# An LRU layer's first blocks fed by chunks of the norm, with the adaLN sums moved behind them

## The chip, the cores and the metric

The kernel runs on one core of one Trainium2 chip. The metric is the device time of one execution in microseconds (us). Of three executions the median was 2819.17 us (2819.03 to 2819.62).

## The reference, cut to what matters

Two layers over 1024 latent tokens and 256 context tokens, width 1024: an RG-LRU mixer, then a Hyena mixer, each followed by a squared-ReLU MLP of width 4096. The change touches the first layer's start, and for a few lines the preparation of the Hyena filters. What is computed there:

```python
mod = cond @ ada_w[0] + ada_b[0]           # six parts: sh1, sc1, g1, sh2, sc2, g2
u = rms_norm(x) * g * (1 + sc1) + sh1      # x: 1024 tokens; the same for the 256 of ctx
z = u @ w_in + b_in                        # 1024 -> gate half and xl half
gate = gelu(z[:, :W]);  xl = conv4(z[:, W:])
r, i = sigmoid(xl_head @ w_a + b_a), sigmoid(xl_head @ w_i + b_i)   # two directions, heads of 256
a = exp(-8 r softplus(-lam));  bx = sqrt(1 - a^2) * i * xl
h = scan(a, bx) in both directions, started from the context's last state
x = x + g1 * (((h_f + h_b) * gate) @ w_out + b_out)
x = x + g2 * mlp(rms_norm(x) * g' * (1 + sc2) + sh2)
```

## The kernel before

Activations stand transposed: channels on the 128 partitions, tokens along the free dimension, in three chunks (0 and 1: 512 latent tokens each, 2: the 256 context tokens). Each product in float32 is made as three matmuls of a rounded part and a remainder (`mm3`, L133): high by high, high by low, low by high. `load` (L111) brings a weight block of 128x1024 by SP's DMA queue into one of two `raw` buffers, ScalarE rounds it into `whi` (L115), VectorE makes the remainder `wlo` (L117). The same two `raw` buffers also take other weights, in program order.

Each instruction's engine is fixed by the code; the order on an engine comes from a planner that simulates the program when it is built (`schedule_with_timeline_sim`), with `high_priority` blocks first. On the chip each engine then works in that fixed order, and an instruction that waits holds up all behind it on its engine. `tc.issue_after(ins)` puts what the block traces behind `ins` on the engine of `ins`, in order only.

The start of the program, in the order of the code:
- `ada_first` (L161) makes the parts 0 and 1 of `mod` (shift and scale of the first norm) for latent and context together: for each part eight blocks of 512 KB of `ada_w`, two matmuls a block with only two weight columns (L174), a row of 2x1024 copied out by ScalarE (L179), eight small transposes (L181), two additions (L183, L184). It is called from `aside` (L1178), between the three rounds of `filter_pos` (L318, the Hyena filter's small network on VectorE and ScalarE). Between the two parts `x_load` brings all of x and ctx, and `norm_stats` works out the three chunks' norms.
- the end of `filter_pos` shuffles the network's output into `hp`, splits it and writes it to DRAM (`hpd`); `filter_w4` (L370) splits 1 MB of `fw4` and writes it to DRAM (`w4d`), for `filters` (L376) to fetch four times in the MLP.
- `lru` (L478) applies the norm, chunk by chunk (`norm_apply`, L282: VectorE L288, ScalarE L290, ScalarE's rounding L291, remainder L292 on GpSimd for even and VectorE for odd blocks).
- then the tokens of L473, one after another. X makes one block of 128 channels of xl (24 matmuls for each chunk, then a convolution on VectorE L527, rounding L547 and remainder L549), Z one block of the gate, U both gates of both directions (it needs both X of its head), A and S the coefficients and the scans, Y fetches finished blocks back for w_out. E (L652) sums one whole part of `mod` on VectorE: eight blocks of 512 KB through `raw`, one multiplication and seven multiply-adds of 128x1024 (L659, L661), then small matmuls (L664).

```python
TOKENS = ("X00 X01 E20 Z00 E30 U00 E40 A00 X10 S00 Z01 U01 A01 X11 S01 "
```

So the first two X, the parts 2, 3 and 4 of `mod`, the first Z and the first U alternate, and every E stands in the same SP queue, `raw` buffers and VectorE and TensorE queues as the blocks around it.

Of the kernel before, what the change touches and what calls it, by code (L numbers as in the profile page):

```python
# [16 lines left out]
P = 128  # L17
# [29 lines left out]
def tile_block(ctx: ExitStack, tc: tile.TileContext, a, out, dbg=None):  # L47
# [49 lines left out]
    w4d = dram.tile([4, P, 2, 512], F32, name="w4d")  # L97
# [64 lines left out]
    def ada_first(pool, wpool):  # L162

        pp = {}

        def step(j, k):
            tag = ("raw", "hi", "lo", "hi", "lo", "raw", "hi", "lo")[k]
            w = wpool.tile([P, 1024], F32R if tag != "raw" else F32, tag=tag, name=nm("afw"), bufs=2 if tag == "raw" else 3)
            w = w.bitcast(F32) if tag != "raw" else w
            nc.sync.dma_start(w, a["ada_w"][0, k * P:(k + 1) * P, j * D:(j + 1) * D])  # L170
            if k == 0:
                pp[j] = [psum(), psum()]
            for h in range(2):
                nc.tensor.matmul(pp[j][h][0:2, :], cond[:, :, k], w[:, h * 512:(h + 1) * 512], start=(k == 0), stop=(k == NT - 1))  # L174
            if k == NT - 1:
                pt = psum()
                for h in range(2):
                    row = pool.tile([P, 512], F32, tag="acc", name=nm("arow"), bufs=1)[0:2]
                    nc.scalar.copy(row, pp[j][h][0:2, :])  # L179
                    for t in range(4):  # L180
                        nc.tensor.transpose(pt[:, 8 * h + 2 * t:8 * h + 2 * t + 2], row[:, t * P:(t + 1) * P], ident[0:2, 0:2])  # L181
                pv = pt[:, 0:16].rearrange("p (t a) -> p t a", a=2)
                nc.vector.tensor_tensor(mod[:, 0, j], pv[:, :, 0], vcols("ada_b", 8 * j, 8), op=ALU.add)  # L183
                nc.vector.tensor_tensor(modc[:, j], pv[:, :, 1], vcols("ada_b", 8 * j, 8), op=ALU.add)  # L184
        return [lambda j=j, k=k: step(j, k) for j in range(2) for k in range(NT)]
# [94 lines left out]
    applied = [None, None]  # L280

    def norm_apply(pool, xs, r, n, scale, shift, uh, ul, inplace=False):  # L282

        rb = r if r.shape[-1] == n else norm_bcast(pool, r, n, 1 if inplace else 2)
        for k in range(NT):
# [4 lines left out]
            nc.scalar.activation(u, t, AF.Identity, scale=scale[:, k:k + 1], bias=shift[:, k:k + 1])  # L290
            nc.scalar.copy(uh[k], u)  # L291
# [26 lines left out]
    def filter_pos(fp, fb, aside):  # L318
# [13 lines left out]
        for n in range(3):  # L332
# [12 lines left out]
            aside(n)  # L345
        tap("fh3", h)
# [8 lines left out]
        hp = fp.tile([P, 16, 4, 32], F32, tag="hp", name="hp")  # L355
        nc.gpsimd.memset(hp, 0.0)
        for half in range(2):
# [5 lines left out]
            for m in range(2):  # L363
                for j in range(4):
                    eng = nc.scalar.copy if j % 2 else nc.vector.tensor_copy
                    eng(dst[:, :, m, (j + m) % 4, 16 * half:16 * half + 16], src[:, :, m, j, :])
        for n, t in enumerate(split(fb, "hps", hp.rearrange("p g j t -> p (g j t)"), [P, 2048], 1, "v")):
            nc.sync.dma_start(hpd[:, :, n].rearrange("g p c -> p g c"), t.bitcast(F32).rearrange("p (g c) -> p g c", g=16))

    def filter_w4(fp, fb):  # L370
        fw4 = fp.tile([P, 2048], F32, tag="fw4", name="fw4")
        nc.sync.dma_start(fw4, a["fw4"])
        for n, t in enumerate(split(fb, "w4s", fw4, [P, 2048], 1)):
            nc.sync.dma_start(w4d[:, :, n].rearrange("u p c -> p u c"), t.bitcast(F32).rearrange("p (u c) -> p u c", u=4))

    def filters(fp):  # L376
# [88 lines left out]
    def x_load(pool):  # L465
        xt = []
        for c, src, o, n in ((0, "xT", 0, 512), (1, "xT", 512, 512), (2, "ctxT", 0, TC)):
            xt.append([pool.tile([P, n], F32, tag=f"x{c}{k}", name=nm("xl"), bufs=1) for k in range(NT)])
            for k in range(NT):
                nc.sync.dma_start(xt[c][k], a[src][k * P:(k + 1) * P, o:o + n])  # L470
        return xt
# [946 lines left out]
```

## Time and profile before

| | |
|---|---|
| median of three executions | 2819.17 us |
| the profiled execution's own time | 2820.53 us |
| its span | 2818.8 us (1.7 us lie around it) |
| TensorE busy | 2664.5 us, 95% |
| VectorE busy | 1519.5 us, 54% |
| ScalarE busy | 1045.7 us, 37% |
| GpSimd busy | 256.6 us, 9% |
| mean granted TensorE clock | 0.97 of full speed |

The profile is one execution. Engines are PE (TensorE, with PEld its weight loads), DVE (VectorE), ACT (ScalarE), POOL (GpSimd) and SP (the queue that issues most DMAs). A matmul's time in the trace is longer than its distance to the next, since they are pipelined; the distance is what counts. "ps L135 <- ACT u L291" says that a matmul of line 135 waited for the ScalarE instruction of line 291.

### The profile page before, as it was taken

Reading aid. Unit: us, or ns where it says so; the run is one execution under the profiler, and the core shown is the slowest. Engines: PE = TensorE matmul, PEld = TensorE weight load, DVE = VectorE, ACT = ScalarE, POOL = GpSimd, SP = SyncE. Lnnn points to the kernel's source line nnn. Section 1 sums busy time; section 2 is a strip of 40 time slices with the busy share of each in tenths; the row PEclk is TensorE's granted clock in tenths of the full one; section 3 lists DMA queues with packets and bytes.
Section 4 is the critical chain, followed back from the end, with each engine's and each line's share of the span. In section 5 each row is a group of like instructions: output and inputs, shape, how many; then the busy total and the mean of one; then the engine's idle time right before and its main releaser. Section 6 shows DMA issues by size and latency. Waiting matters only on the chain. (4 is left out here: it accounts for less than half of the span.)

```text
span 2818.8 us, 30100 instructions
## 1 busy us (share of the span) xinstructions
PE 2664.5 (95%) x11578; PEld 2027.9 (72%) x11578; DVE 1519.5 (54%) x2077; ACT 1045.7 (37%) x1566; POOL 256.6 (9%) x162
## 2 busy tenths in 40 slices
PE   6689898999999999999999998889799999999998
PEld 1577777878777777778787763333588888888887
DVE  7665665874554554554843447547485333333336
ACT  5557577552333333322622233323353221112213
POOL 0223333010000000000100013212000000000000
PEclk8789999999999999999999999999999999999999
DMA  8331122342443443431313235555421111111112
GB/s 302 124 123 40 50 75 100 117 129 75 135 134 114 142 133 110 135 114 57 120 56 111 83 123 150 139 162 160 134 83 48 51 47 51 45 53 45 53 45 97
DMA packets 120272, 286.28 MB, mean 102 GB/s; under 512 B 11898, under 2 KB 27900, under 8 KB 120002
## 3 DMA queue, kind: packets, MB, share of 16 engines
q1 hardware_dynamic: 109618, 261.30, 29.5%
q10 hardware_dynamic: 8256, 14.68, 1.8%
q0 software_dynamic: 2256, 8.39, 0.9%
q8 instruction: 91, 1.49, 0.2%
q14 instruction: 51, 0.42, 0.0%
HBM read 212.76 MB, written 37.75 MB: 89 GB/s over the span
## 5 line engine op out<-in xcount | busy, mean ns | idle before, releaser
L154 PE MATMUL ps<-u,whi 128*128 128x512 f32 x2696 | 733.5, 392 | 0.0
L115 ACT CAST whi<-raw 128x1024 fp32r<-128x1024 f32 x206 | 216.7, 1052 | 1130.8 <-PE ps L154 1033.5
L154 PEld LDWEIGHTS ps<-u,whi 128*128 128x128 f32 x2696 | 504.1, 188 | 114.6 <-DVE x L789 4.2
L117 DVE TENSOR_TENSOR wlo<-raw,whi 128x1024 fp32r<-128x1024 f32 x206 | 262.1, 1272 | 468.7 <-ACT whi L115 467.9
L154 PE MATMUL ps<-u,wlo 128*128 128x512 f32 x1348 | 421.3, 389 | 0.1
L154 PEld LDWEIGHTS ps<-u,wlo 128*128 128x128 f32 x1348 | 252.9, 188 | 53.7 <-DVE wlo L117 0.8
L154 PE MATMUL ps<-hh,whi 128*128 128x512 f32 x896 | 290.6, 393 | 0.0
L154 PE MATMUL ps<-hh,wlo 128*128 128x512 f32 x896 | 288.4, 389 | 0.0
L154 PE MATMUL ps<-hl,whi 128*128 128x512 f32 x896 | 287.7, 390 | 0.0
L154 PEld LDWEIGHTS ps<-hh,whi 128*128 128x128 f32 x896 | 168.2, 188 | 51.4 <-DVE x L789 11.1
L136 PE MATMUL ps<-u,whi 128*128 128x512 f32 (+1 forms) x508 | 195.4, 386 | 3.7 <-POOL u L292 3.1
L135 PE MATMUL ps<-u,whi 128*128 128x512 f32 (+1 forms) x508 | 187.3, 385 | 11.5 <-ACT u L291 11.5
L137 PE MATMUL ps<-u,wlo 128*128 128x512 f32 (+1 forms) x508 | 193.1, 382 | 1.8 <-DVE wlo L117 1.8
L154 PEld LDWEIGHTS ps<-hh,wlo 128*128 128x128 f32 x896 | 168.1, 188 | 35.2
L154 PEld LDWEIGHTS ps<-hl,whi 128*128 128x128 f32 x896 | 167.9, 188 | 33.8
L789 DVE SCALAR_TENSOR_TENSOR big<-ps,mod,big 128x512 f32<-128x512 f32 (+1 forms) x132 | 91.7, 731 | 185.2 <-PE ps L154 177.7
L789 DVE SCALAR_TENSOR_TENSOR x<-ps,mod,x 128x512 f32<-128x512 f32 x128 | 91.4, 747 | 132.8 <-PE ps L154 124.9
L415 DVE TENSOR_TENSOR ht<-ps,ht 128x512 f32<-128x512 f32 x64 | 44.0, 687 | 162.9 <-PE ps L137 162.9
L292 POOL TENSOR_TENSOR u<-nu,u 128x512 fp32r<-128x512 f32 x24 | 33.9, 1412 | 990.6 <-ACT u L291 981.4
L135 PEld LDWEIGHTS ps<-u,whi 128*128 128x128 f32 x508 | 98.0, 194 | 30.1 <-ACT u L291 12.3
L136 PEld LDWEIGHTS ps<-u,whi 128*128 128x128 f32 x508 | 98.2, 193 | 25.6 <-POOL u L292 6.4
L137 PEld LDWEIGHTS ps<-u,wlo 128*128 128x128 f32 x508 | 97.7, 192 | 20.3 <-DVE wlo L117 3.0
(228 smaller groups left out, 3798.2 us busy)
## 6 DMA issues: line engine op xcount, KB each, us to landing
raw<-in_mlp_w_dram SPq DMA_DIRECT2D x136, 512.0 KB
adaw<-in_ada_w_dram SPq DMA_DIRECT2D x112, 256.0 KB
fd<-fe SPq DMA_DIRECT2D x64, 256.0 KB
ft<-fd SPq DMA_DIRECT2D x64, 256.0 KB
e<-big SPq DMA_DIRECT2D x64, 256.0 KB
eraw<-in_ada_w_dram SPq DMA_DIRECT2D x24, 512.0 KB
raw<-in_hy_w_in_dram SPq DMA_DIRECT2D x24, 512.0 KB
big<-e ACTq DMA_DIRECT2D x48, 256.0 KB
```

What stands on the lines that cost most here:

```text
L115: lsplit[0] = nc.scalar.copy(hi, raw)
L117: lsplit[1] = nc.vector.tensor_tensor(lo, raw, hi.bitcast(F32), op=ALU.subtract)
L135: first = pin(nc.tensor.matmul(ps, wh, rh, start=start, stop=False))
L136: pin(nc.tensor.matmul(ps, wh, rl, start=False, stop=False))
L137: pin(nc.tensor.matmul(ps, wl, rh, start=False, stop=stop))
L154: nc.tensor.matmul(pp[c], x, y[c][k], start=first, stop=last)
L292: applied[k % 2] = (nc.vector if k % 2 else nc.gpsimd).tensor_tensor(ul[k], u, uh[k].bitcast(F32), op=ALU.subtract)
L415: nc.vector.tensor_tensor(ht, ps, ht, op=ALU.mult)
L789: last[0] = nc.vector.scalar_tensor_tensor(xs[m][:, cs], ps[:, :n], g2[:, m:m + 1], xs[m][:, cs], op0=ALU.mult, op1=ALU.add)
```

## The change

- `ada_first` gathers two blocks of `ada_w` and issues four matmuls on them, whose results go to partitions 0, 32, 64 and 96 of one PSUM tile; `finish` adds the two halves on VectorE. All sixteen loads come in one run, behind those of chunk 0 of x; chunks 1 and 2 are loaded behind the first three `w_in` blocks.
- The norm is worked out and applied chunk by chunk; of chunk 0 every second block, of the others every fourth, is scaled on VectorE instead of ScalarE. `filter_mat` (the shuffle, split and write of `hp`) stands behind all norms, splits in four pieces, and `filter_w4` is gone: `fetch` splits its part itself.
- A token B takes the place of X00, X01 and Z00: three blocks side by side, chunk by chunk.
- E is replaced. F sums part 3 (inside B) and part 4 (behind U00) as E did, its VectorE instructions behind the last one of `filter_mat`, then of the convolutions (`mixed`); G makes their small matmuls behind the last matmul before. Part 2 is summed late, in steps E00 to E30 between the last Z and U, from half blocks in tiles `u2` that held the context, which Y's fetches use next.
- The pool `lt` allocates its tiles in another order.

```diff
+        def finish(j):
+            row = pool.tile([P, 2, 512], F32, tag="acc", name=nm("arow"), bufs=1)[0:2]
+            pt = psum()
             for h in range(2):
+                nc.scalar.copy(row[:, h], pp[j][32 * h:32 * h + 2])
+                nc.vector.tensor_tensor(row[:, h], pp[j][64 + 32 * h:66 + 32 * h], row[:, h], op=ALU.add)
+                for t in range(4):
+                    nc.tensor.transpose(pt[:, 8 * h + 2 * t:8 * h + 2 * t + 2], row[:, h, t * P:(t + 1) * P], ident[0:2, 0:2])
...
         def fetch(u):
             w = fp.tile([P, 2, 512], F32R, tag="w4", name=nm("w4"), bufs=2)
-            nc.sync.dma_start(w.bitcast(F32), w4d[u])
+            raw = fp.tile([P, 512], F32, tag="fe", name=nm("w4r"), bufs=2)
+            nc.sync.dma_start(raw, a["fw4"][:, u * 512:(u + 1) * 512])
+            nc.scalar.copy(w[:, 0], raw)
+            nc.vector.tensor_tensor(w[:, 1], raw, w[:, 0].bitcast(F32), op=ALU.subtract)
...
-    TOKENS = ("X00 X01 E20 Z00 E30 U00 E40 A00 X10 S00 Z01 U01 A01 X11 S01 "
+    TOKENS = ("B00 U00 F40 G40 A00 X10 S00 Z01 U01 A01 X11 S01 "
...
-              "Z30 U30 A30 Z31 U31 " + ...
+              "E00 Z30 E10 U30 A30 Z31 E20 U31 E30 " + ...
...
+                fs = fst.enter_context(tc.tile_pool(name="fs", bufs=1, reuse_waits="tile"))
+                first, finish = ada_first(fs, wp_[0])
+                h = filter_pos(fs)
+                x_load(xt, 0)
+                for step in first:
+                    step()
                 with tc.high_priority():
+                    for j in (1, 0):
+                        finish(j)
...
+                    w0 = [load(a["lru_w_in"][m]) for m in (8, 9, 0)]
+                for c in (1, 2):
+                    x_load(xt, c)
+                with tc.high_priority():
+                    for c, n in ((0, 512), (1, 512), (2, TC)):
+                        r = norm_stats(npool, lambda k: xt[c][k], n, npool)
+                        norm_apply(..., (rounded[0], applied[1]) if c else (), c == 0)
+                with tc.issue_after(rounded[0].ins), tc.issue_after(applied[0].ins), tc.issue_after(applied[1].ins):
+                    copied = filter_mat(fs, h)
...
+            mm, mixed, sums = [None], [copied], {}
+            def F(j, _):
+                acc = sums[j] = lt.tile([P, T], F32, tag="hf" if j == 3 else "g", name=nm("eacc"), bufs=1 if j == 3 else 2)
+                with tc.issue_after(mixed[0].ins):
+                    for k in range(NT):
+                        w = wp_[0].tile([P, 1024], F32, tag="raw", name=nm("eraw"), bufs=2)
+                        nc.sync.dma_start(w, a["ada_w"][0, k * P:(k + 1) * P, j * D:(j + 1) * D])
...
+            def B(h, m):
+                for c in range(3):
+                    n = 3 if c < 2 else 2
...
+                    for k in range(NT):
+                        for i in range(n):
+                            mm[0] = gemm(pp[i], w0[i], 0, uh[c], ul[c], [k], NT)
+                    for i in range(2):
+                        nc.scalar.activation(zz[i][:, cols[c]], pp[i], AF.Identity, bias=vcol("lru_b_in", 8 + i))
+                    if c < 2:
+                        table(g[:, cols[c]], pp[2], AF.Gelu_apprx_tanh, bias=vcol("lru_b_in", 0))
+                F(3, 0)
+                for i in range(2):
+                    mix(0, i, zz[i])
+                G(3, 0)
...
+            def E(step, _):
...
+                with tc.issue_after(lsplit[1].ins):
+                    for k in range(NT) if 0 < step < 3 else ():
+                        o = acc[:, 512 * (step - 1):512 * step]
...
+                for k in range(NT) if step < 2 else ():
+                    ew[k] = utile("", 2, F32)
+                    c0 = 2 * D + 512 * step
+                    nc.sync.dma_start(ew[k], a["ada_w"][0, k * P:(k + 1) * P, c0:c0 + 512])
+                if step == 3:
+                    ada_sum(2, acc)
```

## Rows read from the trace of the kernel before

**Rows 1.** The page: engines' busy time, its share of the span, and instructions.

```profile
PE 2664.5 (95%) x11578; PEld 2027.9 (72%) x11578; DVE 1519.5 (54%) x2077; ACT 1045.7 (37%) x1566; POOL 256.6 (9%) x162
```

**Rows 2.** Busy time by stretch: the stretch in us, its length, then busy us (and instructions) of each engine, granted clock, DMA share, GB/s. The last two rows are from the layer's middle and end.

```profile
0.00:7.60 7.60, 2.06 (x3) 0.55 (x4) 2.45 (x12) 4.39 (x6) 2.45 (x7) 1.00 0.70 215
7.60:24.00 16.40, 16.40 (x32) 2.88 (x32) 8.33 (x30) 4.31 (x8) 0.00 (x0) 1.00 1.03 396
24.00:39.85 15.85, 6.58 (x30) 4.36 (x29) 13.62 (x33) 13.24 (x27) 0.00 (x0) 0.70 1.02 367
39.85:58.00 18.15, 18.15 (x41) 3.87 (x41) 16.80 (x42) 13.40 (x25) 0.00 (x0) 0.89 0.66 232
58.00:79.60 21.60, 1.97 (x11) 1.21 (x10) 12.17 (x27) 15.06 (x24) 0.49 (x1) 0.57 0.54 168
79.60:110.30 30.70, 30.57 (x144) 25.14 (x144) 24.16 (x22) 16.77 (x34) 15.77 (x12) 0.91 0.26 81
110.30:142.00 31.70, 19.13 (x68) 15.34 (x67) 22.81 (x24) 9.37 (x11) 0.00 (x0) 0.69 0.60 188
142.00:170.97 28.97, 22.66 (x104) 19.96 (x103) 14.22 (x11) 11.87 (x17) 4.55 (x2) 0.74 0.58 182
...
265.00:312.00 47.00, 43.08 (x200) 36.28 (x199) 29.63 (x19) 32.40 (x38) 18.34 (x6) 0.93 0.16 48
...
405.00:450.00 45.00, 39.12 (x173) 32.26 (x172) 31.47 (x22) 28.03 (x36) 12.71 (x4) 0.92 0.21 67
```

**Rows 3.** What TensorE waited for in the first 600 us: us in total, times, longest.

```profile
PE ps L135 <- ACT xh L547: 17.5, 3, 5.9
PE pst L664 <- DVE eacc L661: 17.1, 3, 6.3
PE ps L135 <- ACT u L291: 11.5, 1, 11.5
```

**Rows 4.** TensorE in order of time: start, us, instruction, and in brackets the idle time before it and what ended it. The first X begins in the first row; the last row is the start of X10.

```profile
79.60 1.22 PE L135 MATMUL ps<-u,whi 128*128 128x512 f32 x2 [11.54 <-ACT u L291]
...
80.62 0.63 PE L136 MATMUL ps<-u,whi 128*128 128x512 f32 x1
...
81.05 0.63 PE L137 MATMUL ps<-u,wlo 128*128 128x512 f32 x1
...
100.02 0.39 PE L136 MATMUL ps<-u,whi 128*128 128x512 f32 x1
100.25 0.39 PE L137 MATMUL ps<-u,wlo 128*128 128x512 f32 x1
...
170.97 0.56 PE L135 MATMUL ps<-u,whi 128*128 128x256 f32 x1
```

**Rows 5.** SP's queue in order of time: start, us, what it issues, how many.

```profile
138.72 0.33 SPq L113 DMA_DIRECT2D raw<-in_lru_w_g_dram  x1
141.38 21.21 SPq L657 DMA_DIRECT2D eraw<-in_ada_w_dram  x8
163.58 4.19 SPq L113 DMA_DIRECT2D raw<-in_lru_w_in_dram  x2
```

**Rows 6.** VectorE in order of time: the first step of each of the three E, one of the steps that waited, A00, A01, and the idle time before Y's remainders.

```profile
96.45 0.74 DVE L659 TENSOR_SCALAR eacc<-eraw,cond 128x1024 f32<-128x1024 f32 x1
...
120.01 0.75 DVE L659 TENSOR_SCALAR eacc<-eraw,cond 128x1024 f32<-128x1024 f32 x1
...
134.97 1.28 DVE L661 SCALAR_TENSOR_TENSOR eacc<-eraw,cond,eacc 128x1024 f32<-128x1024 f32 x1 [1.48 <-DMA eraw<-in_ada_w_dram]
137.40 1.28 DVE L661 SCALAR_TENSOR_TENSOR eacc<-eraw,cond,eacc 128x1024 f32<-128x1024 f32 x1 [1.15 <-DMA eraw<-in_ada_w_dram]
...
145.16 0.75 DVE L659 TENSOR_SCALAR eacc<-eraw,cond 128x1024 f32<-128x1024 f32 x1
...
223.02 2.89 DVE L613 SCALAR_TENSOR_TENSOR T<-r,T 128x1280 f32<-128x1280 f32 x2 [4.70 <-ACT r L567]
...
445.11 2.73 DVE L648 TENSOR_TENSOR u<-u,u 128x512 fp32r<-128x512 f32 x4 [11.02 <-ACT u L647]
```

**Rows 7.** Groups of instructions by line in the first 171 us: busy us, mean ns of one, idle time before them and what ended it.

```profile
L174 PE MATMUL ps<-afw,cond 128*2 128x512 f32 x64 | 32.8, 669 | 1.4 <-DMA afw<-in_ada_w_dram 1.4
...
L292 DVE TENSOR_TENSOR u<-xl,u 128x512 fp32r<-128x512 f32 (+1 forms) x12 | 14.4, 1260 | 11.3 <-ACT u L291 11.3
...
L341 DVE SCALAR_TENSOR_TENSOR fs<-fk,fs 128x512 f32<-128x512 f32 x9 | 6.2, 688 | 0.0
L117 DVE TENSOR_TENSOR wlo<-raw,whi 128x1024 fp32r<-128x1024 f32 x5 | 6.1, 1223 | 3.8 <-ACT whi L115 3.7
...
L179 ACT COPY arow<-ps 2x512 f32<-2x512 f32 x4 | 2.3, 571 | 4.6 <-PE ps L174 3.0 <-PE ps L181 1.6
L315 DVE TENSOR_TENSOR hpsl<-hp,hpsh 128x2048 fp32r<-128x2048 f32 x1 | 2.3, 2284 | 0.0
L315 DVE TENSOR_TENSOR w4sl<-fw,w4sh 128x2048 fp32r<-128x2048 f32 x1 | 2.3, 2275 | 0.0
```

**Rows 8.** The same over the whole span, shapes apart: small matmuls on 32 of the array's rows and columns, several of them under way together.

```profile
L432 PE MATMUL ps<-ht,mf 32*32 32x512 f32 x512 | 34.8, 600 | 0.0
```

**Rows 9.** Line 292 on GpSimd: shortest, median and longest in ns, then first and last start. First the MLP's and Hyena's norms, then the LRU's.

```profile
L292 POOL TENSOR_TENSOR u<-nu,u x24: 1273/1296/2511, 563.8 to 2132.0; 128x512 fp32r<-128x512 f32 x24
...
L292 POOL TENSOR_TENSOR u<-xl,u x12: 918/1376/1747, 79.1 to 95.1; 128x512 fp32r<-128x512 f32 x8, 128x256 fp32r<-128x256 f32 x4
```

More of the change, by code (lines that the diff above doesn't have):

```diff
@@ L175, in step @@
[L175 to L184, printed above, removed]
@@ L187, in ada_half @@
+        return [lambda j=j, k=k: step(j, k) for j in range(2) for k in range(NT)], finish
     def ada_half(pool, l, j, h):
@@ L279, in tile_block, with norm_apply @@
     spread = [None]
-    applied = [None, None]
-    def norm_apply(pool, xs, r, n, scale, shift, uh, ul, inplace=False):
+    applied, rounded = [None, None], [None]
+    def norm_apply(pool, xs, r, n, scale, shift, uh, ul, inplace=False, after=(), even=False):
         rb = r if r.shape[-1] == n else norm_bcast(pool, r, n, 1 if inplace else 2)
@@ L289, in norm_apply @@
             u = x if inplace else pool.tile([P, 512], F32, tag="nu", name=nm("nu"), bufs=2)
-            nc.scalar.activation(u, t, AF.Identity, scale=scale[:, k:k + 1], bias=shift[:, k:k + 1])
-            nc.scalar.copy(uh[k], u)
+            with ExitStack() as order:
+                for ins in after:
+                    order.enter_context(tc.issue_after(ins.ins))
+                if inplace and (k % 2 == 0 if even else k % 4 == 1):
+                    nc.vector.tensor_scalar(u, t, scale[:, k:k + 1], shift[:, k:k + 1], op0=ALU.mult, op1=ALU.add)
+                else:
+                    nc.scalar.activation(u, t, AF.Identity, scale=scale[:, k:k + 1], bias=shift[:, k:k + 1])
+            rounded[0] = nc.scalar.copy(uh[k], u)
             applied[k % 2] = (nc.vector if k % 2 else nc.gpsimd).tensor_tensor(ul[k], u, uh[k].bitcast(F32), op=ALU.subtract)
@@ L344, in filter_pos, with filter_mat @@
             nc.scalar.activation(h, s, AF.Sin)
-            aside(n)
-        tap("fh3", h)
+        return h
+    def filter_mat(fp, h):
         lo, up = h[0:64], h[64:128]
@@ L354, in filter_pos @@
         nc.vector.tensor_copy(hh[64:128, 511:1023], up)
-        hp = fp.tile([P, 16, 4, 32], F32, tag="hp", name="hp")
+        hpr = fp.tile([P, 2048], F32R, tag="hp", name="hp")
+        hp = hpr.bitcast(F32).rearrange("p (g j t) -> p g j t", g=16, j=4)
         nc.gpsimd.memset(hp, 0.0)
+        copied = [None]
         for half in range(2):
@@ L365, in filter_pos @@
                     eng = nc.scalar.copy if j % 2 else nc.vector.tensor_copy
-                    eng(dst[:, :, m, (j + m) % 4, 16 * half:16 * half + 16], src[:, :, m, j, :])
-        for n, t in enumerate(split(fb, "hps", hp.rearrange("p g j t -> p (g j t)"), [P, 2048], 1, "v")):
-            nc.sync.dma_start(hpd[:, :, n].rearrange("g p c -> p g c"), t.bitcast(F32).rearrange("p (g c) -> p g c", g=16))
[L370 to L374, printed above, removed]
+                    ins = eng(dst[:, :, m, (j + m) % 4, 16 * half:16 * half + 16], src[:, :, m, j, :])
+                    copied[0] = copied[0] if j % 2 else ins
+        hph = fp.tile([P, 2048], F32R, tag="hph", name="hph")
+        for q in range(4):
+            cs = slice(512 * q, 512 * q + 512)
+            nc.scalar.copy(hph[:, cs], hpr[:, cs].bitcast(F32))
+            nc.gpsimd.tensor_tensor(hpr[:, cs], hpr[:, cs].bitcast(F32), hph[:, cs].bitcast(F32), op=ALU.subtract)
+        for n, t in enumerate((hph, hpr)):
+            nc.sync.dma_start(hpd[:, :, n].rearrange("g p c -> p g c"), t.bitcast(F32).rearrange("p (g c) -> p g c", g=16))
+        return copied[0]
     def filters(fp):
@@ L1169, in tile_block @@
     npool = npst.enter_context(tc.tile_pool(name="ln", bufs=1, side="right", reuse_waits="tile"))
[L1170 to L1192 removed]
+    xs, r0 = lru(load, open_x, npool, npst.close)
     for k in range(NT):
```

114 lines of the change are left out of this document (59 added, 55 removed).

## The prediction

> **What bounds the kernel now.** The page first: TensorE is busy 95% of the span and no other engine over 54% [rows 1], so a change to the rest pays only where TensorE stands still. The stretches show where: up to 79.60 us the layer's first product has not begun, and from 110.30 to 170.97 TensorE is busy 19.13 of 31.70 and 22.66 of 28.97 us, at granted clocks of 0.69 and 0.74; in the layer's middle it is 43.08 of 47.00 at 0.93 [rows 2]. By columns the work done from 79.60 to 170.97 (X00, X01, Z00, U00) is small. At the full clock a 512-column matmul follows the one before by 0.23 us, at the half clock by 0.43 [rows 4]; X and U are 24 matmuls for each of two and a half chunks (24 x 2.5 x 0.23 = 13.8 us), Z is 24 x 2 x 0.23 = 11.0, together 52 us in a stretch of 91. The waits name who holds it: first the rounded norm (11.5 us, once), then three times the sums of E (17.1 us) [rows 3].
>
> The queue and VectorE show how E holds it. E's eight blocks go through two `raw` buffers, so a step comes every 2.4 us (134.97, 137.40) though VectorE works 1.28 of it and then waits for the DMA [rows 6]. U00's weights, queued behind eight such blocks, are issued at 138.72, 18.7 us after that E's first step at 120.01; eight more follow over 21.21 us, and X10's at 163.58 [rows 5, 6]. X10 starts at 170.97 [rows 4], 25.8 us after the last E's first step at 145.16 [rows 6]. So three sums in a row, begun at 96.45, set X10's start. From there the layer repeats units of one Z, U, A, X and S (38.6 us of matmuls by the sum above, 47 with the waits, of which the longest is for `xh` [rows 2, 3]). I take what is gained before X10 as kept.
>
> **The change, part by part.** I sum from the profiled execution, 2820.53 us (span 2818.8 and 1.7 around it), which lies 1.4 above the median 2819.17.
>
> *Packed adaLN matmuls and loads.* Before the last block of parts 0 and 1 there now come 16 x 0.52 MB, chunk 0 of x at 2.1 MB, and 0.5 MB of small inputs: 11.0 MB. At the rates of the first stretches, 215 GB/s for 7.6 us and 396 for 16.4 bring 8.1 MB by 24.0, and 367 the last 2.9 in 7.9 us [rows 2]: 32 us. TensorE needed 32.8 us for these 64 matmuls [rows 7]; small matmuls on separate parts of the array took 34.8 us for 512, 0.07 each where one lasts 0.60 [rows 8], so four side by side should stay behind the DMA. `finish` is a chain for each part: two copies at 0.57 [rows 7], two additions, by the nearest VectorE row of that width 0.69 [rows 7], transposes and small operations, 3.5 us with handovers, twice because of one `row` tile: 39 us. One scaling and one rounding later, at 42, the first matmul of B can run, where X00 ran at 79.60. Its three weight blocks, issued behind the adaLN's, need 1.6 MB more, 4.3 us at 367 GB/s, and hide in `finish`.
>
> *B.* Chunks 0 and 1 with three blocks cost 24 x 3 x 0.23 = 16.6 us each, the context with two 5.5. The first 5 us at the half clock add 2.5, as from 79.60. B could end at 83 if the norms of chunks 1 and 2 keep ahead.
>
> *VectorE, which decides more than B.* F waits behind `filter_mat`, and that behind all norms. What VectorE does before E's first step adds up to 2.45 + 8.33 + 13.62 + 16.80 + 12.17 in the stretches to 79.60 [rows 2] and 14.4 in L292 [rows 7]: 67.8 us. Gone are the splits of `fw4` and `hp`, 2.3 each, and the rounding of `hp`, taken at a `wlo`'s 1.2 [rows 7]; new are four additions at 0.69, eight scalings at about 0.4 (half a 1024-column step of 0.75 [rows 6]) and a third `wlo` at 1.2 [rows 7]: 69 us. If VectorE never waits from 3 us on, F begins at 72; if it waits as now, at 96.45 as E did. The data arrive earlier and the chunks overlap, but the norms' chains (sum, square root, spread) remain in line: I take 85, the middle.
>
> *F and G, two sums instead of three.* F3 goes through the same two `raw` buffers ahead of U00's weights, F4 ahead of X10's. So: F3's first step at 85, U00's weights issued 18.7 later at 103.7, F4's first step 6.4 after that (145.16 - 138.72), X10 25.8 later: 135.9 against 170.97, a gain of 35.1. The bounds of 72 and 96.45 give gains of 48 and 23.6. B's convolutions (some 13 us of VectorE) lie beside F3 as X01's did beside E. U00 starts about 109 and is done before X10; TensorE stands idle on either side, and these restarts at the half clock lie inside the durations taken from before. Behind F's waiting step on VectorE stand the convolutions that U00 needs, behind U00's weights on SP the loads of F4: both are in the distances used.
>
> *From X10 to A01.* That took 52.0 us (170.97 to 223.02) [rows 4, 6], with A00's and S00's VectorE work inside. Now A00 ends before X10. X10, Z01 and U01 are 38.6, A01's first operations some 7 more; against this the second buffer of `g` now belongs to F4, so Z01's result waits for S00's last product. I take 3 of the 6.5 us; bounds 0 and 6.5.
>
> *Part 2 at the end of the layer.* Two multiplications and fourteen multiply-adds of 512 columns, 10.4 us at 0.4 and 0.69; VectorE is busy 31.47 of 45.00 us there and stands idle 11.02 before Y's remainders [rows 2, 6]. Y's fetches now wait until these steps free the `u2` tiles. I take 1 us of loss; bounds 0 and 41 (below).
>
> *`fetch` in the MLP, the order in `lt`, the early write of `hpd`.* Four copies at about 0.6 and four subtractions at 0.69 [rows 7] beside the MLP's matmuls, against one DMA of half the size: I take 0, bounds -2 and 4 (all four in line). A tile of `lt` over the last bytes of the old pool could wait for `hpd`; that wait ends about when U00's weights come, so 0.
>
> The sum: 2820.5 - 35.1 - 3 + 1 = 2783.4; less 1.4, 2782 for the median.
>
> Two rules weighed, which nothing above needs. On GpSimd the median remainder took 1.30 us in quiet norms and 1.38 beside the first one, with 1.75 the longest [rows 9]. The Trainium skill's page "GPSIMD Engine Reference", section "8. Key points", says that GpSimd shares its SBUF interfaces with VectorE and loses time to VectorE instructions that use two ports or two SBUF inputs; this agrees in direction, and by it the eight scalings moved to VectorE could each hold a remainder up for their 0.4 us, 3 us in all, an estimate that would make the sum 2785. A step of E took 2.4 us [rows 6]; by the fit of the Trainium skill's page "DMA: Bandwidth & Descriptors", section "Anatomy of one DMA — SWDGE (gpsimd) path", 2.0 us and 436 GB/s, a block takes 3.2 us, and two buffers with 1.28 us of work each give 2.2 a step, an estimate by which sixteen steps would end 3 us earlier and the sum be 2779. That fit is for GpSimd's path and these loads are SP's; the measured step stands.
>
> **The rivals.**
> 1. VectorE hardly waits: F begins near 74, A01 keeps all of its 6.5 us. For it: all of x and ctx, 15.7 MB with the weights, is there by 45 us at the rates above; against it: VectorE was idle 28.6 of its first 96.45 us [rows 2, 7]. Gain 46 + 6.5 - 1 = 51: 2768.
> 2. The norms stay in line as before (squares, sums and spreads of chunk 1 are queued in TensorE's and VectorE's fixed order behind data that come late), F begins at 96.45, and only one of three sums is gained: 23.6 less 1: 2797. For it: the order comes from a simulation. Against it: the scale that the norms wait for is there at 39, and chunk 0 no longer waits for the others.
> 3. The packing doesn't do what it says: the four matmuls run one after another, 32.8 us from about 13, when chunk 0 and two blocks (3.7 MB) have landed, and `finish` begins at 46 rather than 33. VectorE has work meanwhile, so I count 10 of the 13: 2792. Rows 8 speak against it, though for a smaller tile.
> 4. Slower: the late sum of part 2 becomes the chain. If each of its sixteen half blocks waits for its own DMA at 2.4 us a step (no prefetch, as `u2` tiles come free one at a time), it takes 39 us, and Y's fetches, the first `w_out` product and the small matmuls stand behind it, with 7 us for Y's fetch, rounding and a restart at the half clock. A price of 46 against a gain of 38: 2828. It decides from 38 us on. Against it: eight tiles are free together, and VectorE had time there [rows 6].
>
> **How the numbers follow.** The forecast 0.50 (its own range 2774 to 2790), rival 1 0.20, rival 2 0.14, rival 3 0.09, rival 4 0.07; of rival 4 0.04 is slower and 0.03 within the bound, as its price may fall short. The time is the forecast's, 2782. The range runs from 2760, which takes in rival 1 with the bound of 72 (2765) and a faster `fetch`, to 2806, rival 2 with 9 us for `fetch` and Y; beyond it lie rival 4 and mixtures, below 0.2. The runs before differ by 0.02%; I take 0.2%, 5.6 us, as the least that a measurement tells from no change. Faster by more: 0.92; within: 0.04; slower: 0.04.
>
> **What would show it.** The first `w_in` matmul near 42 us; B's end near 83 to 90; F's first step between 72 and 96; U00's weights 18 to 19 us behind it; X10 near 136; A01's first multiply-add near 185 instead of 223.02; the following units 47 us apart as before; `w_out` as far behind the last U as now. The forecast is wrong if X10 starts before 122 or after 150, if F doesn't hold U00's weights, or if the distance from A01 to the MLP's start changes by more than 5 us.

## The result, and the profile after

The changed kernel takes 2797.75 us (median of 4 runs, 2795.33 to 2799.75) against 2819.1 (4 runs, 2816.98 to 2819.62): a ratio of 0.9925, interval 0.9908 to 0.9943. That is 21 us faster where 37 were forecast. Beside the experiments further below the kernel before was run again, with medians of 2814.3 to 2816.3, so times from different experiments are compared by their ratios and not as they stand. The profiled execution took 2799.75 us with a span of 2798.0.

The page's engine line, as [rows 1]:

```profile
PE 2640.9 (94%) x11578; PEld 2022.7 (72%) x11578; DVE 1530.6 (55%) x2098; ACT 1040.1 (37%) x1563; POOL 263.0 (9%) x166
```

Busy time by stretch, as [rows 2]: stretch, length, busy us and instructions of PE, PEld, DVE, ACT and POOL, granted clock, DMA share, GB/s. The borders are the first `w_in` matmul (67.08), the end of B (108.26), the first matmul of U00 (123.70), X10 (149.79) and A01 (200.95).

```profile
24.00:39.40 15.40, 10.95 (x48) 1.90 (x48) 13.93 (x27) 7.71 (x17) 0.00 (x0) 1.00 1.02 367
39.40:67.08 27.68, 12.32 (x52) 5.51 (x53) 22.17 (x56) 14.65 (x28) 0.00 (x0) 0.60 0.38 130
67.08:108.26 41.18, 41.18 (x192) 34.45 (x192) 26.94 (x31) 29.46 (x57) 23.08 (x17) 0.94 0.27 84
108.26:123.70 15.44, 3.44 (x17) 3.44 (x17) 15.12 (x18) 6.74 (x9) 0.00 (x0) 0.66 0.59 185
123.70:149.79 26.09, 18.96 (x89) 16.49 (x90) 15.39 (x11) 13.64 (x19) 7.30 (x2) 0.83 0.60 181
149.79:200.95 51.16, 50.51 (x242) 43.06 (x243) 32.86 (x23) 32.94 (x39) 15.98 (x5) 0.92 0.22 73
```

B runs without a gap. Behind it TensorE stands idle and VectorE is full (15.12 of 15.44 us): the small matmuls of G3, ahead of U00 on TensorE, wait for VectorE. TensorE's waits up to 600 us, as [rows 3], and those of SP's queue up to 300:

```profile
PE pst L761 <- DVE eacc L586: 19.1, 2, 12.0
PE ps L134 <- ACT xh L611: 17.4, 3, 5.9
...
PE ps L189 <- DVE arow L187: 7.8, 4, 4.0
PE ps L134 <- ACT g L652: 5.5, 1, 5.5
```

```profile
SPq L392 <- ACT hph L389: 32.8, 1, 32.8
```

The wait for the sums (pst) is not smaller than the 17.1 us of before: two waits in place of three, one of them 12 us. SP stands 32.8 us at the `hpd` write, with six of F3's eight loads behind it, as its queue shows [rows 5]:

```profile
6.55 6.19 SPq L171 DMA_DIRECT2D afw<-in_ada_w_dram  x8
13.70 9.52 SPq L493 DMA_DIRECT2D xl<-in_xT_dram  x8
23.57 5.09 SPq L493 DMA_DIRECT2D xl<-in_ctxT_dram  x8
28.77 4.30 SPq L171 DMA_DIRECT2D afw<-in_ada_w_dram  x8
...
55.66 4.95 SPq L582 DMA_DIRECT2D eraw<-in_ada_w_dram  x2
93.47 0.39 SPq L392 DMA_DIRECT2D hpd<-hph  x1
97.39 0.37 SPq L392 DMA_DIRECT2D hpd<-hp  x1
97.86 16.39 SPq L582 DMA_DIRECT2D eraw<-in_ada_w_dram  x6
117.07 0.33 SPq L112 DMA_DIRECT2D raw<-in_lru_w_g_dram  x1
120.23 9.67 SPq L582 DMA_DIRECT2D eraw<-in_ada_w_dram  x4
```

VectorE [rows 6]: first inside `finish`, then from F3's first step to F4's. L570 are the convolutions' steps, L586 the sum's.

```profile
47.26 4.87 DVE L296 TENSOR_TENSOR xl<-xl,prb 128x512 f32<-128x512 f32 x8 [0.26 <-PE prb L284]
...
53.82 0.69 DVE L187 TENSOR_TENSOR arow<-ps,arow 2x512 f32<-2x512 f32 x1
...
55.66 2.74 DVE L296 TENSOR_TENSOR xl<-xl,prb 128x256 f32<-128x256 f32 x8
58.44 0.69 DVE L187 TENSOR_TENSOR arow<-ps,arow 2x512 f32<-2x512 f32 x1
...
90.39 0.75 DVE L584 TENSOR_SCALAR eacc<-eraw,cond 128x1024 f32<-128x1024 f32 x1
...
104.67 1.29 DVE L586 SCALAR_TENSOR_TENSOR eacc<-eraw,cond,eacc 128x1024 f32<-128x1024 f32 x1 [12.21 <-DMA eraw<-in_ada_w_dram]
105.88 1.25 DVE L570 SCALAR_TENSOR_TENSOR xc<-z,vec,xc 128x992 f32<-128x992 f32 x1
107.04 1.28 DVE L586 SCALAR_TENSOR_TENSOR eacc<-eraw,cond,eacc 128x1024 f32<-128x1024 f32 x1
...
124.23 1.49 DVE L613 TENSOR_TENSOR xl<-xc,xh 128x1280 fp32r<-128x1280 f32 x1
125.64 0.75 DVE L584 TENSOR_SCALAR eacc<-eraw,cond 128x1024 f32<-128x1024 f32 x1
...
200.95 2.89 DVE L698 SCALAR_TENSOR_TENSOR T<-r,T 128x1280 f32<-128x1280 f32 x2 [4.70 <-ACT r L652]
```

And ScalarE's eviction of B's `z`, which lies over the end of `hph` and waits until `hpd` is written:

```profile
98.65 1.27 ACT L630 ACTIVATE z<-ps,vec 128x512 f32<-128x512 f32 x2 [5.20 <-DMA hpd<-hph]
```

So F3 does two steps, waits 12.21 us for a load behind the `hpd` writes, and then shares VectorE with both convolutions until 125.6. F4 repeats this ahead of X10. The gain over before is 12.5 us at the first `w_in` matmul, 6.1 at F's first step, 21.2 at X10, 22.1 at A01 (223.02 to 200.95), then only 15.8 at the first step of the MLP's norm.

### The profile page after: what moved, and what is told of

Read it like the earlier page. It is cut to its first block, busy times and chain, and to the rows that moved or that the text cites. A ratio compares the mean times of both kernels' runs of the same rounds, so it can differ in the third digit from the quotient of the medians.

```text
span 2798.0 us, 30133 instructions
## 1 busy us (share of the span) xinstructions
PE 2640.9 (94%) x11578; PEld 2022.7 (72%) x11578; DVE 1530.6 (55%) x2098; ACT 1040.1 (37%) x1563; POOL 263.0 (9%) x166
## 4 chain that ended last, share of the span: by engine, by line
PE 78%; DVE 7%; DMA 7%; ACT 5%; issue 2%; POOL 1%; SPq 0%; DVEq 0%; ACTq 0%; POOLq 0%
PE ps L153 56%; PE ps L134 4%; PE ps L135 4%; PE ps L136 4%; DMA e<-big 3%; DMA big<-e 2%; PE ps L1095 1%; PE ps L1055 1%; PE ps L1071 1%; PE ps L1076 1%; PE ps L454 1%; DVE xc L570 1%; PE ps L961 1%; DMA eraw<-in_ada_w_dram 1%; DVE hf L715 1%
```

## The experiments

The table has the starts read from each run's trace (us), and each run's ratio to runs of the kernel before made beside it. "w_g" are U00's weights. A01 counts for the layer's start, the norm for the whole layer; where an expectation names A5 or A6, these are the sixth and seventh unit, A21 and A30. The first line after "changed" has the changed kernel's order of instructions and starts 0.6 to 0.8 us earlier throughout: about that much lies between two profiles of one kernel. In "part 2 early" the column F3 has the first step of F2, which comes ahead of it.

| run | first w_in | F3 | w_g issued | U00 | X10 | A01 | MLP's norm | ratio, interval |
|---|---|---|---|---|---|---|---|---|
| before | 79.6 | (E) 96.5 | 138.7 | 144.9 | 171.0 | 223.0 | 560.9 | |
| changed | 67.1 | 90.4 | 117.1 | 123.7 | 149.8 | 201.0 | 545.0 | 0.9925, 0.9908 to 0.9943 |
| z off hph | 66.3 | 89.6 | 116.4 | 123.0 | 149.1 | 200.1 | 544.4 | 0.9930, 0.9917 to 0.9944 |
| hpd by GpSimd | 67.0 | 90.3 | 124.0 | 128.6 | 156.9 | 207.7 | 551.2 | 0.9961, 0.9949 to 0.9974 |
| both | 65.9 | 89.3 | 116.7 | 121.3 | 152.1 | 202.5 | 546.2 | 0.9941, 0.9929 to 0.9954 |
| no part 2 | 66.0 | 89.3 | 116.0 | 122.6 | 149.4 | 199.8 | 537.1 | 0.9916, 0.9903 to 0.9930 |
| no F3 | 66.0 | none | 54.5 | 111.4 | 144.1 | 193.9 | 538.0 | 0.9912, 0.9897 to 0.9927 |
| x late | 58.6 | 93.1 | 119.7 | 126.4 | 153.1 | 203.5 | 547.4 | 0.9945, 0.9930 to 0.9959 |
| unpacked | 69.4 | 93.4 | 119.8 | 126.4 | 152.2 | 203.5 | 547.2 | 0.9945, 0.9930 to 0.9960 |
| no chunks | 66.5 | 89.8 | 121.2 | 127.3 | 152.9 | 204.2 | 548.5 | 0.9950, 0.9934 to 0.9967 |
| F deep | 66.1 | 89.4 | 109.9 | 120.8 | 136.5 | 193.2 | 537.3 | 0.9911, 0.9898 to 0.9925 |
| F deep, x late | 57.6 | 91.9 | 106.0 | 118.0 | 136.5 | 188.3 | 532.0 | 0.9894, 0.9879 to 0.9909 |
| part 2 early | 66.3 | 89.6 | 138.1 | 144.2 | 170.9 | 221.7 | 558.9 | 0.9994, 0.9985 to 1.0003 |
| Y late | 57.4 | 91.9 | 106.0 | 118.0 | 136.5 | 188.3 | 530.9 | 0.9897, 0.9881 to 0.9914 |

### The two waits beside the hpd write

**z off hph:**

```diff
-            fk = fp.tile([P, 512], F32, tag="fk", name=nm("fk"), bufs=2)
+            fk = fp.tile([P, 512], F32, tag="fk", name=nm("fk"), bufs=1)
```

> Edit: the filter kernel's tile fk has one buffer in place of two, so that everything behind it in the pool fs lies 2 KB lower and the tile z of lt no longer lies over the end of hph; the order of instructions is the changed kernel's on every engine. Theory A (two things bind at once: z waits for the read of hph by the hpd write, 5.20 us at 98.65, and VectorE's sum F3 waits 12.21 us for a load that stands behind the two hpd writes on SP): z's eviction comes at once, but U00's weights are still held by F3, so the issue of w_g stays near 117 and X10 near 150 us; the end moves by 0 to 3 us from the changed kernel's 2797.8. Rival (the overlap of z alone held U00): X10 comes about 5 us earlier, near 145, and the end near 2793.

**hpd by GpSimd:**

```diff
-            nc.sync.dma_start(hpd[:, :, n].rearrange("g p c -> p g c"), ...
+            nc.gpsimd.dma_start(hpd[:, :, n].rearrange("g p c -> p g c"), ...
```

> Edit: the two hpd writes are issued by GpSimd in place of SP, so F3's third load doesn't stand behind them. Theory A (both bind): F3's 12.21 us wait for its load goes, w_g is issued near 105 to 109 us in place of 117.07; the convolutions still wait for z until about 105 and xl comes near 122, so U00 begins at most 1 to 3 us earlier; X10 near 148 and the end near 2796. Rival B (the SP queue alone held U00): X10 near 142 and the end near 2790. Rival C (F3's load is late for another reason, as the transfers of x chunks and w_in still run): the 12.21 us wait stays and so does the end, 2798.

**Both:**

> Edit: both of the edits above. Theory A: z comes at once and w_g is issued near 107; U00 begins some 8 us earlier, X10 near 142, the end near 2790. If one of the two was the whole cause, this run equals that run. If neither was (the chain of evictions behind U00 sets X10), X10 stays near 150 and the end near 2798.

Each edit takes its wait away. In the first, `z` was evicted at 92.67, but F3's third step still came at 103.97. In the second, that step came at 95.08, but GpSimd wrote `hpd` later and held `z` until 105.15: 7 us worse at X10. With both, VectorE's order around F3 is this:

```profile
93.92 2.14 DVE L586 SCALAR_TENSOR_TENSOR eacc<-eraw,cond,eacc 128x1024 f32<-128x1024 f32 x1 [2.60 <-DMA eraw<-in_ada_w_dram]
102.61 1.25 DVE L570 SCALAR_TENSOR_TENSOR xc<-z,vec,xc 128x992 f32<-128x992 f32 x1 [6.55 <-ACT xc L567]
103.78 1.28 DVE L586 SCALAR_TENSOR_TENSOR eacc<-eraw,cond,eacc 128x1024 f32<-128x1024 f32 x1
```

F3's fourth step stands behind the first convolution step, which waits for `z`'s second chunk (its matmuls end near 99). The weights are issued at 116.7, against 117.1 in the changed kernel. Theory A (both waits together are the cause) predicted 107 and falls; the case that neither is, with X10 near 150 and the end near 2798, holds (152.1 and 2798.0). Something third ends at the same time.

### F3's price

**No F3:**

```diff
-                F(3, 0)
...
-                G(3, 0)
+                nc.vector.tensor_copy(mod[:, 0, 3], vcols("ada_b", 24, 8))
```

> Left out: the sum F3 and its closing G3 (eight loads of eraw, eight VectorE steps, eight small matmuls); the bias alone stands for part 3 of adaLN, so the numbers behind it are others. Theory A, as it stands now (U00 waits for VectorE, which has 12 convolution steps, two remainders and F3's last five or six steps between z's second chunk at about 100 us and U00): without F3 the convolutions end near 113, U00 begins near 115 instead of 123.8, X10 near 140 instead of 150, the end near 2788. Rival (F3 costs nothing, B's late start alone sets U00): U00 stays within 2 us of 123.8 and the end near 2797.

U00 comes 12.3 us earlier, X10 5.7, A01 7.0. So F3 holds U00, as forecast; but the convolutions still begin at 103.29 there, when `z`'s second chunk is there:

```profile
103.29 1.25 DVE L570 SCALAR_TENSOR_TENSOR xc<-z,vec,xc 128x992 f32<-128x992 f32 x1 [14.05 <-ACT xc L567]
```

F4 then waits behind them, so that taking out a second sum gains much less than the third sum costs (below, "part 2 early").

### What of the start brings how much

**x late:**

```diff
-                for c in (1, 2):
-                    x_load(xt, c)
...
+                with tc.issue_after(afw[0].ins):    # the last adaLN load
+                    for c in (1, 2):
+                        x_load(xt, c)
```

> Edit: the loads of x chunk 1 and of ctx are issued behind the last of the 16 adaLN blocks, not between the two parts. Theory A (the forecast missed the first w_in matmul by 25 us because the chunks' loads and norms stand ahead of finish on SP and VectorE, and B's start carries through to U00): finish ends near 50 instead of 63, the first w_in matmul comes near 53 instead of 67, z's second chunk near 90, U00 near 114, X10 near 141, the end near 2789. Rival V (VectorE's work in sum is the bound, the norms only change places): the first w_in matmul comes as early, but F3's first step stays at 88 to 92 and X10 at 148 to 152, the end near 2798.

The first `w_in` matmul came 8.5 us earlier and F3 2.7 later, X10 3.3 later: rival V, a little beyond its bounds. The norms of chunk 1 and ctx only change places with `finish` on VectorE, and F waits for all of them. TensorE's wait for `z` over `hph` shows that B's earlier start was lost here too:

```profile
102.10 0.58 PE L134 MATMUL ps<-u,whi 128*128 128x256 f32 x1 [6.87 <-ACT z L633]
```

**Unpacked:** (the four additions of `finish` go too)

```diff
-            for i in (0, 1):
-                for h in range(2):
-                    r = 64 * i + 32 * h
-                    nc.tensor.matmul(pp[j][r:r + 2, :], cond[:, :, k - 1 + i], ws[k - 1 + i][:, h * 512:(h + 1) * 512], ...
+            for h in range(2):
+                nc.tensor.matmul(pp[j][h][0:2, :], cond[:, :, k], w[:, h * 512:(h + 1) * 512], ...
```

> Edit: the packing alone undone: parts 0 and 1 as 64 matmuls into two rows of two PSUM tiles, without the four additions of finish on VectorE. Theory A (the loads set the pace of these matmuls, and VectorE the length of finish): the last of them ends within 1 us of 48.8, finish is up to 2.8 us shorter, X10 is 0 to 3 us earlier and the end 2795 to 2798. Rival (the packing is what brings the matmuls to the pace of the loads): the last ends 10 us later, X10 near 158 and the end near 2806.

The groups by line up to 70 us, first unpacked, then the changed kernel (busy us, mean ns, idle time before):

```profile
L176 PE MATMUL ps<-afw,cond 128*2 128x512 f32 x64 | 30.1, 623 | 0.0
```

```profile
L180 PE MATMUL ps<-afw,cond 128*2 128x512 f32 x64 | 14.3, 702 | 1.3 <-DMA afw<-in_ada_w_dram 1.3
```

Unpacked, the last of them ends at 58.5, ten microseconds after the packed kernel's 48.8, as the rival said. But its `finish` takes 7 us against 14.6, because without the additions it needs VectorE only once, at its end, and the first `w_in` matmul comes only 2.3 us later. Neither theory had that in full.

**No chunks:** B computes X00 over all chunks, then X01, then Z00.

```diff
-                for c in range(3):
-                    n = 3 if c < 2 else 2
...
+                for i in range(3):
+                    for c in range(3 if i < 2 else 2):
```

> Edit: B's chunk order alone undone: the same three weight blocks, but X00 over all three chunks, then X01, then Z00. Theory A: X00's last chunk waits for the norm of ctx until about 86, TensorE stands idle 10 us or more before it and B ends near 114 to 118 instead of 108.26; the convolutions of X00 begin near 92, those of X01 near 105, so U00 begins 0 to 4 us later than 123.8, and the end is 2797 to 2802. Rival (the chunk order is what the gain consists of): U00 begins 10 us later or more, the end is at 2808 or above.

U00 3.6 us later, as expected; but B ends at 110.38, not at 114 to 118: the norms keep ahead of TensorE even so. Undoing the packing, the chunk order or the order of the loads costs 2.6 to 3.2 us each at A01 by the traces; the intervals of their ratios overlap the changed kernel's.

### What removes F from the way

**F deep**, on "both":

```diff
-                        w = wp_[0].tile([P, 1024], F32, tag="raw", name=nm("eraw"), bufs=2)
+                        t = (("raw", "raw", "T", "T", "xl2", "raw", "T", "raw") if j == 3 else ("T", "T", "xl2", "raw", "raw", "T", "T", "raw"))[k]
+                        if t == "raw":
+                            w = wp_[0].tile([P, 1024], F32, tag="raw", name=nm("eraw"), bufs=2)
+                        else:
+                            w = lt.tile([P, T + TC], F32 if t == "T" else F32R, tag=t, name=nm("eraw"), bufs=2 if t == "T" else 1)
+                            w = (w if t == "T" else w.bitcast(F32))[:, :T]
```

> Edit: F3's and F4's loads go through five buffers in place of two (the two of raw, the two of T and the one of xl2, which stand empty then), fk has one buffer and the hpd writes are GpSimd's, as in the run with both. Theory A (F's loads and its steps between the convolutions hold U00, and F4 holds X10, 24 us from its first step): F3 has four steps done before the first convolution at about 102, U00 begins near 119 in place of 123.8, F4's eight steps take 11 to 13 us instead of 21, X10 comes near 139 instead of 150, the end near 2787. Rival B (the second chunk of z at 100 us and the convolutions behind it set U00, and U00's own evictions set X10): U00 near 120 but X10 not before 146, the end near 2794. Rival C (the wider prefetch takes DMA bandwidth from nothing that counts and the steps are VectorE's): no change, 2798.

```profile
90.19 5.76 DVE L591 SCALAR_TENSOR_TENSOR eacc<-eraw,cond,eacc 128x1024 f32<-128x1024 f32 x3
103.24 1.25 DVE L570 SCALAR_TENSOR_TENSOR xc<-z,vec,xc 128x992 f32<-128x992 f32 x1 [7.30 <-ACT xc L567]
...
123.60 7.89 DVE L591 SCALAR_TENSOR_TENSOR eacc<-eraw,cond,eacc 128x1024 f32<-128x1024 f32 x6
132.57 1.28 DVE L591 SCALAR_TENSOR_TENSOR eacc<-eraw,cond,eacc 128x1024 f32<-128x1024 f32 x1 [1.08 <-DMA eraw<-in_ada_w_dram]
```

F4's eight steps now run one behind the other, 122.81 to 133.85. X10 follows U00's last matmul at once, at 136.5, which is where the forecast had put it; the planner also put the small matmuls of G4 behind X10's start here, at 139.5. The time is 2790.52 us (ratio 0.9911, against 0.9941 for "both"). Of the 13.3 us that X10 gains on the changed kernel, 7.7 reach A01: U00 itself came only 2.9 earlier, held by the convolutions, which begin at 103.24 with `z`'s second chunk.

**F deep, x late:** the same with the edit of "x late".

> Edit: as the run before it, and the loads of x chunk 1 and ctx behind the adaLN's last block. That edit alone brought the first w_in matmul 8.4 us forward and X10 3.3 us back. Theory A (alone it was covered by the wait for F's load and by z over hph, both gone here): z's second chunk comes near 93 in place of 100, U00 near 114, X10 near 134, the end near 2782. Rival V (the norms of chunk 1 and ctx on VectorE, which end 3 us later with this edit, hold F and the convolutions): X10 0 to 4 us later than in the run without the edit, near 141, the end near 2789.

The first line is ScalarE's eviction of `z`'s second chunk in "F deep", the second in this run:

```profile
100.03 1.37 ACT L635 ACTIVATE z<-ps,vec 128x512 f32<-128x512 f32 x2 [4.30 <-PE ps L136]
```

```profile
98.14 1.26 ACT L638 ACTIVATE z<-ps,vec 128x512 f32<-128x512 f32 x2
```

The edit that alone cost 2.6 us at A01 gains 5.0 here. 2785.95 us (0.9894) is 29.8 below the runs of before beside it (2815.79), where the changed kernel was 21.4 below its own; its interval and the changed kernel's just touch, and the traces have A01 12.7 us and the norm 13.0 us ahead of the changed kernel. `z`'s second chunk comes at 98.14 instead of 100.03, not at 93 as expected, U00 starts at 118.0, not 114, and X10 does not move (136.54). What moves behind it is A00, whose first multiply-add comes at 142.19 instead of 147.02, and with it A01. That is theory A in its direction, about half its size, and not at X10. So three things ended within a few microseconds of each other: F's loads and steps, `z` over `hph`, and B's start. Taking one or two away showed nothing, or a loss. Whether the deeper F would do without the first two edits was not tried.

### What the gain consists of, and what is given back

**Part 2 early:** all of the change stays but this.

```diff
+                F(2, 0)
                 F(3, 0)
...
+                G(2, 0)
                 G(3, 0)
...
-              "E00 Z30 E10 U30 A30 Z31 E20 U31 E30 "
+              "Z30 U30 A30 Z31 U31 "
```

> Edit: part 2's sum alone is put back to the layer's start, as F2 and G2 ahead of F3 and G3 in B, and E00 to E30 are gone from the end. Theory A (most of the change's gain is that one of three sums left the way to X10, at 2.4 to 2.6 us for each of eight steps, and 5 us of it is given back at the layer's end): X10 comes 19 to 22 us later, near 171, A01 near 222, A6 about 5 us nearer than that, the end near 2813. Rival (the gain comes from B, the packing or the norms; a third sum hides beside the convolutions): X10 0 to 8 us later, the end at 2792 to 2800.

X10 comes at 170.89, 0.08 us from the kernel before; the ratio is 0.9994. X10's start, then TensorE's waits for the sums:

```profile
170.89 0.56 PE L134 MATMUL ps<-u,whi 128*128 128x256 f32 x1
```

```profile
PE pst L763 <- DVE eacc L586: 36.0, 3, 17.6
```

With the third sum back, nothing is left at X10 of the packing, of B and of the rounding order: F2 begins 6.8 us before the old first E (89.63 against 96.45), and the wait for its third load, 12.39 us here, takes that back. So what pays in this kernel is that one of three sums left the way. That wait is the change's own, by the `hpd` writes; three sums with the deeper buffers were not run, so what the earlier start is worth without the wait is shown only by the 5.0 us of "F deep, x late".

**No part 2:** what its late place costs. The sum of part 2 is left out; part 2 is g1 of the reference, the gate of the mixer itself, not of the MLP as the expectation has it.

```diff
+                if step == 3:
+                    nc.vector.tensor_copy(mod[:, 0, 2], vcols("ada_b", 16, 8))
+                return
                 if step == 0:
```

> Left out: the sum of the MLP-side part 2 of the adaLN product (its loads, multiply-adds and the matmuls that close it, the steps E00 to E30), the bias alone stands in its place, so the numbers behind it are others. Theory T (the late sum costs the 5 to 6 us by which the gain over the kernel before falls between unit A5 and A6): A6 comes 21 to 22 us ahead of the kernel before in place of 16.7, and the end near 2792. Rival (the loss there comes from something else, such as Z31 or the order of loads of u): A6 and the end stay, 2797 to 2799.

From A01 to the MLP's norm the changed kernel takes 344.1 us, this one 337.3, the kernel before 337.9 and "part 2 early" 337.2: part 2's place at the layer's end costs 6 to 7 us. A30 comes 23.8 us ahead of the kernel before in place of 16.7. At the MLP's norm "no part 2" is 7.9 us ahead of the changed kernel, 1.1 of it from A01; its time, 2791.81 us, is 4.1 below that of "z off hph" beside it.

**Y late**, on "F deep, x late":

```diff
...
-                nc.scalar.copy(h_, y)
+                with tc.issue_after(tanh[0].ins):    # the second Tanh of the unit last built
+                    nc.scalar.copy(h_, y)
```

> Edit: as the run with the deeper F and the late x chunks, and Y's roundings on ScalarE are put behind unit A30's two Tanh in the order. Theory T (the layer's end loses 5 us because ScalarE, in its fixed order, waits 8 us for the first u<-yd load, which part 2's half blocks keep from the u2 tiles, and A30's Tanh and Exp and Z31's eviction stand behind it): ScalarE has no such wait ahead of the Tanh, A6 comes 32 to 35 us ahead of the kernel before in place of 29.8, and the end near 2782. Rival (VectorE, with part 2's sixteen steps ahead of Y's remainders and A30's first step, is what is late): A6 moves by less than 1.5 us and the end stays near 2786.

The first line is ScalarE in the changed kernel, standing 7.99 us for Y's first load; then ScalarE in this run:

```profile
430.38 0.62 ACT L732 CAST u<-u 128x512 fp32r<-128x512 f32 x1 [7.99 <-DMA u<-yd]
```

```profile
412.76 1.06 ACT L114 CAST whi<-raw 128x1024 fp32r<-128x1024 f32 x1 [3.75 <-DMA u<-in_ada_w_dram]
413.71 0.47 ACT L660 ACTIVATE r<-ps,vec 128x256 f32<-128x256 f32 x1
414.08 2.61 ACT L660 ACTIVATE T<-r,sp 128x1280 f32<-128x1280 f32 x2
...
423.01 0.62 ACT L742 CAST u<-u 128x512 fp32r<-128x512 f32 x1 [2.58 <-DMA u<-yd]
```

Tanh begins at 414.08, 6.4 us earlier than without the edit, but Exp only 1.0, and 1.0 us is gained at A30 and 1.1 at the norm: the rival. Five roundings now stand between Tanh and Exp and wait there for the same late loads. The time, 2785.26 us (0.9897), is the same as without the edit. That the loads are late because of part 2 is shown by "no part 2", where SP issues Y's first load at 373.9 and its rounding waits for nothing; in the changed kernel SP issues it at 425.56, behind the last half block (424.90). Whether the `u2` tiles or SP's order holds it is open; a run that gave Y other tiles was not tried.

## Why the prediction was right in sign and short in size

- **What bounds it**: right. Sums gate U00 and X10; "no F3" and "F deep" show it, and "part 2 early" shows the gain to be one sum less.
- **The first `w_in` matmul at 42**: 67.08. The loads were taken as in line with their use, with only chunk 0 among them. The code has chunk 1 and ctx behind the `w_in` blocks, but SP issued them between the two adaLN parts (13.70 and 23.57, against 28.77 for the second part), so that the last packed matmul ended at 48.8, not 32. `finish` took 14.6 us, not 7: its additions stand behind 7.6 us of norm products and 3.6 of `wlo` on VectorE. This error cost nothing as the kernel stands: "x late" took 8.5 us of it away and gained nothing. With the deeper buffers the same edit gained 5.0 at A01.
- **B's 41 us**: 41.18.
- **F's first step at 85** (bounds 72 to 96.45): 90.39. VectorE's work to there was put at 69 us and measured 73.5, with 16.9 idle.
- **U00's weights 18.7 us behind it: the step that failed.** They came 26.7 behind. The distance was taken from a stretch in which four of X01's six convolution steps stood among the sum's steps and the loads ran on. The text has B's convolutions lie beside F3 "as X01's did beside E", but B makes two blocks of xl at once, and seven of their twelve steps came before the weights. The text also said that the wait of a tile of `lt` for `hpd` "ends about when U00's weights come, so 0". It did not see that the `hpd` writes also stand in F's own queue: 12.21 us. Without these waits the distance stays 27.5 ("both"), since ten of the convolution steps then come between, behind `z`'s second chunk; with more buffers as well it is 20.5. So the writes alone don't explain it.
- **F4 6.4 behind, X10 25.8 behind that**: 8.6 and 24.2. X10's gain is 21.2 in place of 35.1: 5.4 from F's start and 8.0 from the failed distance, and the other 0.5 from these two.
- **From X10 to A01, a gain of 3 us**: 0.9, within its bounds.
- **Part 2's late sum, 1 us (0 to 41)**: 6 to 7 us, by A01 to the norm. This is one of the text's own signs of being wrong, a change of more than 5 us from A01 to the MLP (344.1 against 337.9); X10, at 149.79, lies just inside another, 150.
- **`fetch`, 0**: the MLP and the filters, from the MLP's norm to the first product of Hyena's long convolution, took 1102.5 us against 1102.8.

All the errors of size point the same way: 13.9 us at X10, 2.1 behind it and 5 at the layer's end turn the forecast gain of 37 into the 15.8 at the MLP's norm. That the time lies nearer to the forecast than this comes from 4.9 us behind the norm, which the prediction did not have (below).

The rivals: the first (VectorE hardly waits) fails, with 16.9 us idle ahead of F and 0.9 us kept from X10 to A01. The second gave 2797, next to the result, with "only one of three sums is gained" for its price; but its condition, F at 96.45, did not occur. That the time came out there is luck: one sum's worth remained for another reason, the wait for F's load and the convolutions. The third is refuted by the two groups of adaLN matmuls. The fourth's mechanism is there at 6 to 7 us instead of 46: the sixteen half blocks came eight at a time.

Of the two rules weighed, the one on GpSimd was sized wrongly. The medians of [rows 9] mix tiles of 512 and 256 columns. Apart, the eight of 512 took 1.63 us in the mean here and 1.55 before, and the four of 256 0.83 against 1.06; twelve together took 16.3 us against 16.7, so nothing of the 3 us came. The first line is from the kernel before, the second from the changed one:

```profile
L292 POOL TENSOR_TENSOR u<-xl,u 128x512 fp32r<-128x512 f32 x8 | 12.3, 1554 | 76.7 <-ACT u L291 76.1 <-POOL u L292 0.6
```

```profile
L306 POOL TENSOR_TENSOR u<-xl,u 128x512 fp32r<-128x512 f32 x8 | 12.8, 1629 | 67.8 <-ACT u L305 67.8
```

Four of the eight scalings were done at 65.5, before the first remainder on GpSimd began at 67.1. What costs time in these rows is remainders on both engines side by side, which both kernels have (last section). The Trainium skill's page "GPSIMD Engine Reference", section "8. Key points", names this case too, VectorE instructions with two SBUF inputs, and the trace agrees. The other rule would have made a step of the sum shorter than the measured 2.4 us, which the prediction kept: F4's first seven steps came 2.4 to 2.8 us apart.

One part stays open. From the MLP's norm to the end, the profiled execution of before took 2257.9 us, the changed kernel 2253.0, and "part 2 early", whose time equals that of before, 2253.5. The other runs' profiles have 2249.2 to 2253.2 there. So these 4.9 us may well belong to that one execution of before, which at 2820.53 lies above all its other runs on record (2812.8 to 2819.6), rather than to the change; the gain would then be nearer to the 15.8 us at the norm than to 21. "z off hph", with the changed kernel's order, was 18.6 below the kernel before beside it. No second profile of the kernel before settles this.

## What to carry to other kernels

A distance between two instructions, taken from a trace, holds only while the same work stands between them on the same queues: list what every queue will hold there, writes included, before using it. When an edit that removes a plain wait changes nothing, look for a second and a third path that end within a few microseconds, and remove them together before calling the wait harmless. A sum that was fed through two buffers cost what its loads took, 2.4 us a step and more for 1.28 us of arithmetic; the empty tiles of a later pool served as further buffers.

## What the runs showed of the hardware

- The 64 two-row adaLN matmuls were busy for 14.3 us packed by four, at the loads' pace, and 30.1 one after another.
- The two 1 MB `hpd` writes issued by GpSimd landed 6.8 and 9.0 us after issue, beside F's loads. Behind the same writes on SP, F3's third load, issued at 97.86, was used at 104.67.
- A remainder of 128x512 took VectorE 1.77 us beside one on GpSimd and 0.68 with GpSimd at rest; on GpSimd it took 1.73 to 1.75 us in the middle of a row of such on VectorE (68.34 to 73.47 in the changed kernel) and 1.30 in the median of the quiet norms [rows 9]. VectorE's two lines are from "x late", where GpSimd worked on remainders from 61.57 to 64.73 and then rested until 74.16:

```profile
63.51 1.77 DVE L308 TENSOR_TENSOR u<-xl,u 128x512 fp32r<-128x512 f32 x1
...
66.34 0.68 DVE L308 TENSOR_TENSOR u<-xl,u 128x512 fp32r<-128x512 f32 x1
```
